# A two-block network on one core: head norms by transposes, retention scores issued a step ahead, three small tiles padded, dense weights split 512 columns at a time

## The chip, the cores and the metric

The kernel runs on one core of a Trainium2 chip. The metric is the device time of one execution, in microseconds (us); the time of a kernel is the median of its runs. TensorE is called PE in the profile, VectorE DVE, ScalarE ACT, GpSimd POOL and SyncE SP.

## The reference, cut to what matters

One sequence of 512 tokens of width 1024 goes through two blocks, all of it in float32. The first block has two layers; each is a mixer and then a feed-forward part, with a layer norm behind each. The mixer projects the tokens and gives each quarter of the width to another recurrence:

```python
p = einsum('btd,dc->btc', h, w_in[l])
pa, pb, pc, pd = _split(p, MIXER_COLS)
ya = _hgrn2_mixer(pa, ...)           # gated linear recurrence, then a norm per head
yb = _gla_mixer(pb, ...)             # the same form, other gates
yc, v_first = _rwkv7_mixer(pc, ...)  # w0 + tanh(w_lr) @ w2, a0 + a_lr @ a2, kk / norm(kk), norm per head
yd = _retnet_mixer(pd, ...)          # (q k^T * decay) v, norm per head
mix = einsum('btc,cd->btd', concatenate([ya, yb, yc, yd]), w_out[l])
h = _layer_norm(DN_ALPHA * h + mix, ...)
f = _swiglu(h, ...) if l == 0 else _moe(h, ...)   # 2816 wide; or 8 experts of 1408, 2 a token
h = _layer_norm(DN_ALPHA * h + f, ...)
```

The norms per head are over 64 values, so a vector of 256 channels has four of them for each token. The second block is a SwiGLU of width 2816, a hybrid mixer (a gated recurrence and a sliding-window attention), and another SwiGLU of width 2816, each with a norm before and behind it.

## The kernel before

**Number format and matmuls.** A float32 product is made of three matmuls of a faster format: every operand is split into a high part and the rest of it (`split`, L350: ScalarE writes `hi` at L352, VectorE `lo` at L353). `mm3` (L381) issues high by high, high weights by low data, low weights by high data (L383 to L385), always with weights of 128x128 and 512 tokens streaming, or 256 where the tokens are taken in halves. `gemm_fm` (L387) sums `nk` such blocks in one PSUM bank; `head_steps` (L433) does the first four outputs of a stage side by side (L443, L444, L446); `gemm_halves` (L404) does the last outputs of a stage with one half of the tokens `lag` blocks behind the other.

**Weights.** A `Stream` (L641) loads raw weights of 128x1024 with SP's queue (L661, a ring of three) and cuts each into pieces of WC=256 columns, each with its own split. Pieces lie in two rings of WB=10 tiles, `whi` and `wlo`, or, for the last units of three stages, in a pool of the stage's own (`wx`). A block of 128 columns is a part of a piece. The experts have a stream of their own (`mhi`, `mlo`, pieces of 1024 columns). Tiles of a pool stand one behind the other in a partition of SBUF, so a small tile's size sets where those behind it begin.

**Stages in time** (us of the profiled execution): mixer of layer 0 to 365, its output projection and layer norm to 415, the first SwiGLU's gate and up projections (operands `xH`, `xL`) to 650 and its down projection (operands `hH`, `hL`) to 765; mixer of layer 1 from 785 to 1140; routing to 1210; eight experts to 1790; second SwiGLU to 2180 (down from 2055 on); hybrid mixer to 2380; third SwiGLU to 2725 (down from 2600 on).

**Order in the mixers of the first block.** `mixer1` (L1489) weaves three chains of generators by costs that their `yield`s state and by weights (`weave`, L782): RWKV (`rwkv_pair` 0 and 1), the projections of all parts, and `hg(0)`, `hg(1)`, `ret`. What is issued on an engine stays in that order. Where all three have work, the projection's large matmuls stand between the small ones of the recurrences.

**What the diff touches there.** `params` (L864) makes small per-channel tiles, `om` the first of them. `head_rstd` (L906) takes squared values `sq` (128 channels, that is two heads, by 512 tokens) and returns in PSUM one factor per head and token, over that head's 64 rows. It is called 10 times in each layer. It sums with four matmuls that use the data as weights (L911), takes Sqrt and reciprocal of 128x8 values (`rstd`, L450: ScalarE L452, VectorE L453; or VectorE's maximum first), and spreads them with eight matmuls by the identity (L922). `self.bones` holds 64x64 blocks of ones on its diagonal; `ident` is the identity. `rwkv_pair` (L1008) makes the decay from one low-rank matmul (`y`, L1021, rows 0 to 63) and, after the decay's chain, the gate from another (L1035, rows 64 to 127). `ret` (L1453) takes pairs of heads j and key tiles jt in turn: scores of two heads on PE, multiplied by a decay matrix `rd` on VectorE (L1471), then two matmuls into `po` (L1474), in the same step.

**The other places.** `tail` is one of the tiles that the router keeps to the end (`Moe.keep`, L1572), and `snk` a small tile of the hybrid mixer in the pool that holds its outputs `yh`, `yl`. The halves of the down projections lie 12 blocks apart (`LAG`, `LAG1`) in the first two SwiGLUs, 18 (`LAG2`) in the third. In `moe_down` the matmul of the rest slots (L2059) has 32 weight columns, in one of four strips of 32 rows in turn.

Of the kernel before, what the change touches and what calls it, by code (L numbers as in the profile page):

```python
# [10 lines left out]
F32R = mybir.dt.float32r  # L11
I32 = mybir.dt.int32
AF = mybir.ActivationFunctionType
OP = mybir.AluOpType
# [4 lines left out]
T = 512  # L19
D = 1024  # L20
P = 128
NT = T // P
# [11 lines left out]
HALF = (slice(0, HT), slice(HT, T))  # L34
WB, WR, WC = 10, 3, 256
HEAD = 4
MR, MW, SHARE = 5, 4, (0, 3, 6)
DECAY_C = math.exp(-0.5)
# [602 lines left out]
class Stream:  # L641
# [22 lines left out]
    def pieces(self, raw):  # L664
        self.units += 1
        return [self.piece(raw[:, c:c + WC]) for c in range(0, 1024, WC)]

    def unit(self):
        return self.ready.pop(0) if self.ready else self.pieces(self.raw())

    def piece(self, raw):
        k = self.K
        if self.pool and self.units > self.own:
            t = self.pool.tile([P, 2, WC], F32R, name="wx", tag="wx", bufs=self.bufs)
            hi, lo = t[:, 0], t[:, 1]
        else:
            hi = k.ws.tile([P, WC], F32R, name="whi", tag="whi", bufs=WB)
            lo = k.ws.tile([P, WC], F32R, name="wlo", tag="wlo", bufs=WB)
        k.split(raw, hi, lo)
        return hi, lo  # L680

    def block(self):
        if self.j == 8:
            self.cur, self.j = self.unit(), 0
        c = self.j * P
        hi, lo = self.cur[c // WC]
        self.j += 1
        return hi[:, c % WC:c % WC + P], lo[:, c % WC:c % WC + P]

# [112 lines left out]
class Mix:  # L802
# [33 lines left out]
    def small(self, n, c):  # L836
        return self.cp.tile([P, c], F32, name=n)
# [26 lines left out]
    def params(self):  # L864
        nc, k, l = self.nc, self.k, self.l
        V = nc.vector
        sm = self.small
        mu = k.par(f"mu{l}")
        self.om = sm("om", 9)
        V.tensor_scalar(self.om, mu, -1.0, 1.0, op0=OP.mult, op1=OP.add)  # L870
# [35 lines left out]
    def head_rstd(self, sq, eps, floor=None):  # L906

        k, nc = self.k, self.nc
        s = k.bankB()
        for i in range(NT):  # L910
            nc.tensor.matmul(s[:, 2 * i:2 * i + 2], sq[:, i * P:(i + 1) * P], k.cA("hsel"), start=True, stop=True)  # L911
        r = k.sm.tile([P, 2 * NT], F32, name="hr")
        if floor is None:
            k.rstd(r, s[:, :2 * NT], eps, 1.0 / 64)
        else:
            nc.vector.tensor_scalar(r, s[:, :2 * NT], floor, None, op0=OP.max)
            nc.scalar.activation(r, r, AF.Sqrt)
            nc.vector.reciprocal(r, r)
        R = k.bankB()
        for i in range(NT):  # L920
            for h in range(2):
                nc.tensor.matmul(R[64 * h:64 * h + 64, i * P:(i + 1) * P],  # L922
                                 r[:, 2 * i + h:2 * i + h + 1].to_broadcast([P, 64]), k.ident, start=True, stop=True)
        return R
# [83 lines left out]
    def rwkv_pair(self, p):  # L1008
# [10 lines left out]
        r, kr = self.x[p], self.x[2 + p]  # L1019
        y = k.bankB()  # L1020
        mm(y, w2[:64, sl], self.x[6][:64], start=True, stop=True)  # L1021
        yield 0.9
        lw = self.a("lw")
        act(lw, y, AF.Tanh, bias=self.hw0[:, p:p + 1], scale=0.5)
# [8 lines left out]
        V.tensor_copy(pe, ch(Pm)[:, :, 63])  # L1033
        y = k.bankB()
        mm(y, w2[64:128, sl], self.x[6][64:128], start=True, stop=True)  # L1035
        yield 0.9
        ta = self.a("ta")
        act(ta, y, AF.Tanh, bias=self.ha0[:, p:p + 1], scale=0.5)
        kt = self.a("kp")
# [413 lines left out]
    def ret(self):  # L1453
# [3 lines left out]
        qk, vt, _ = self.reti  # L1457
        for j in range(2):
            po = k.bankB()
            rd = [self.a("rd") for _ in range(2)]  # L1460
            for h in range(2):
                nc.gpsimd.dma_start(rd[h], k.A["rd"][2 * j + h])
            for jt in range(NT):
                n = T - jt * P
                ss = []
                for h in range(2):
                    rs = slice(64 * h, 64 * h + 64)
                    b = k.bankB()
                    mm(b[:, :n], qk[2 + j][rs, jt * P:(jt + 1) * P], qk[j][rs, jt * P:], start=True, stop=True)
                    s = self.a("Sr")  # L1470
                    V.tensor_tensor(s[:, :n], b[:, :n], rd[h][:, :n], op=OP.mult)  # L1471
                    ss.append(s)
                for h, s in enumerate(ss):
                    mm(po[64 * h:64 * h + 64, jt * P:], vt[:, jt, (2 * j + h) * 64:(2 * j + h + 1) * 64], s[:, :n], start=jt == 0,  # L1474
                       stop=jt == NT - 1, skip_group_check=True)
                yield 1.8
            o, R = self.a("ro"), self.a("rr")
# [87 lines left out]
class Moe:  # L1565
# [37 lines left out]
    def route(self, sT, tot, ap, hot):  # L1603
# [126 lines left out]

        self.tail = self.keep("tail", [P, NT])
        V.tensor_scalar(self.tail, slot[:, :, NE - 1], -float(NS - C), None, op0=OP.add)
# [519 lines left out]
class Hybrid:  # L2252


    def __init__(self, k, s2, big, pool):
# [6 lines left out]
        nc.scalar.dma_start(self.wbd.rearrange("p a b -> p (a b)"), k.A["wbd"])  # L2262
        self.snk = small("snk", 8)
        nc.gpsimd.dma_start(self.snk, k.A["snk"].to_broadcast([P, 8]))
# [269 lines left out]
```

## Time and profile before

| | |
|---|---|
| median of three runs | 2736.74 us (2735.06 to 2743.05) |
| the profiled execution, its own time | 2746.0 us |
| its span, from the first to the last instruction | 2744.2 us |
| its mean granted TensorE clock | 0.982 |
| PE, DVE, ACT, POOL busy | 97%, 61%, 49%, 12% of the span |
| moved by DMA | 333.83 MB, mean 122 GB/s |

The profile is of one execution, a little longer than the median of the three timed ones. Busy time is that in which an engine executes an instruction. Matmuls are pipelined: a record of 0.39 us is followed by the next record some 0.23 us later, so the rate is read from start to start, or by counting records in a window. The name ahead of "MATMUL" is the PSUM tile written, behind the arrow stand the two operands read. A "x4" behind a row of the timeline says that four records in a row were put together. The 40 slices of the page are 68.6 us each.

### The profile page before, as it was taken

To read this page: it belongs to the slowest core of one execution; us is meant where nothing else is said; L and a number is where in the kernel's file an instruction comes from. 1 tells how busy PE (TensorE), PEld (TensorE's weight loads), DVE (VectorE), ACT (ScalarE), POOL (GpSimd) and SP (SyncE) were. 2 spreads that over 40 slices of the span, in tenths; PEclk is the share of its full clock that TensorE was granted. 3 is DMA by queue.
4 is the path that set the end of the run, shared out by engine and by line. 5 is a ranking of instruction groups with operands and counts; after the bars stand their busy time and mean duration, and the time that the engine had idled before them with its cause. 6 is when DMAs were issued, how large, how long until landed. Compare 5 with 4: busy or idle time off the path is not lost. (4 is left out here: it accounts for less than half of the span.)

```text
span 2744.2 us, 48736 instructions
## 1 busy us (share of the span) xinstructions
PE 2661.5 (97%) x18914; PEld 2166.6 (79%) x18914; DVE 1665.4 (61%) x3372; ACT 1335.9 (49%) x2769; POOL 328.1 (12%) x388
## 2 busy tenths in 40 slices
PE   8999999999999999988999999999999999999998
PEld 6777688888877776786888888768888877888887
DVE  7554465443466554456888888965553477755533
ACT  5455335433343553345666777554443367544432
POOL 1000110000030000024333322500000100100000
PEclk9999999999999999989999999989999999999999
DMA  4111413222321112238877777712222212223222
GB/s 165 41 55 48 147 62 101 100 97 95 108 79 41 55 48 70 65 119 272 285 270 271 276 276 274 253 50 100 93 99 93 87 62 65 90 93 100 94 98 70
DMA packets 95788, 333.83 MB, mean 122 GB/s; under 512 B 11825, under 2 KB 15057, under 8 KB 95552
## 3 DMA queue, kind: packets, MB, share of 16 engines
q1 hardware_dynamic: 87424, 306.00, 33.4%
q0 software_dynamic: 7552, 23.96, 2.4%
q8 instruction: 152, 2.49, 0.4%
q10 hardware_dynamic: 576, 0.69, 0.1%
q14 instruction: 84, 0.69, 0.1%
HBM read 313.95 MB, written 17.18 MB: 121 GB/s over the span
## 5 line engine op out<-in xcount | busy, mean ns | idle before, releaser
L352 ACT ACTIVATE whi<-wraw 128x256 fp32r<-128x256 f32 x1164 | 473.5, 415 | 811.8 <-PE bkA L384 751.1
L353 DVE TENSOR_TENSOR wlo<-wraw,whi 128x256 fp32r<-128x256 f32 x1164 | 483.9, 424 | 619.9 <-ACT whi L352 601.5
L383 PE MATMUL bkA<-xH,whi 128*128 128x512 f32 x1352 | 541.4, 400 | 2.6 <-DVE sh L947 2.1
L384 PE MATMUL bkA<-xL,whi 128*128 128x512 f32 x1352 | 533.8, 395 | 0.0
L385 PE MATMUL bkA<-xH,wlo 128*128 128x512 f32 x1352 | 531.9, 393 | 0.0
L1904 PE MATMUL bkA<-xe,mhi 128*128 128x320 f32 x1408 | 365.1, 345 | 3.7 <-ACT mhi L352 2.2
L383 PEld LDWEIGHTS bkA<-xH,whi 128*128 128x128 f32 x1352 | 254.3, 188 | 70.8 <-issue 15.2
L384 PEld LDWEIGHTS bkA<-xL,whi 128*128 128x128 f32 x1352 | 254.7, 188 | 58.2 <-issue 9.6
L385 PEld LDWEIGHTS bkA<-xH,wlo 128*128 128x128 f32 x1352 | 254.5, 188 | 56.3 <-issue 4.2
L1906 PE MATMUL bkA<-xe,mlo 128*128 128x160 f32 x1232 | 292.3, 237 | 3.3 <-DVE mlo L353 3.3
L353 DVE TENSOR_TENSOR mlo<-mraw,mhi 128x1024 fp32r<-128x1024 f32 x165 | 232.9, 1413 | 45.0 <-ACT mhi L352 42.9
L1904 PEld LDWEIGHTS bkA<-xe,mhi 128*128 128x128 f32 x1408 | 254.8, 191 | 5.0 <-ACT mhi L352 2.5
L1906 PEld LDWEIGHTS bkA<-xe,mlo 128*128 128x128 f32 x1232 | 237.5, 193 | 4.7 <-DVE mlo L353 4.5
L383 PE MATMUL bkA<-hH,whi 128*128 128x512 f32 (+1 forms) x548 | 207.0, 378 | 0.0
L384 PE MATMUL bkA<-hL,whi 128*128 128x512 f32 (+1 forms) x548 | 206.7, 377 | 0.0
L385 PE MATMUL bkA<-hH,wlo 128*128 128x512 f32 (+1 forms) x548 | 206.5, 377 | 0.0
L352 ACT ACTIVATE mhi<-mraw 128x1024 fp32r<-128x1024 f32 x165 | 173.2, 1052 | 18.5 <-PE bkA L2066 14.6
L353 DVE TENSOR_TENSOR mlo<-wraw,mhi 128x1024 fp32r<-128x1024 f32 x99 | 131.4, 1327 | 33.8 <-ACT mhi L352 31.3
L384 PEld LDWEIGHTS bkA<-hL,whi 128*128 128x128 f32 x548 | 103.0, 188 | 21.0
L383 PEld LDWEIGHTS bkA<-hH,whi 128*128 128x128 f32 x548 | 103.0, 188 | 21.0
L385 PEld LDWEIGHTS bkA<-hH,wlo 128*128 128x128 f32 x548 | 102.9, 188 | 20.9
L352 ACT ACTIVATE mhi<-wraw 128x1024 fp32r<-128x1024 f32 x99 | 104.5, 1056 | 13.0 <-PE bkA L2066 7.7
(717 smaller groups left out, 4414.3 us busy)
## 6 DMA issues: line engine op xcount, KB each, us to landing
mraw<-moew SPq DMA_DIRECT2D x165, 512.0 KB, 5.3
wraw<-moew SPq DMA_DIRECT2D x99, 512.0 KB, 4.5
wraw<-win SPq DMA_DIRECT2D x76, 512.0 KB, 3.7
wraw<-f0gu SPq DMA_DIRECT2D x44, 512.0 KB, 3.2
wraw<-f1gu SPq DMA_DIRECT2D x44, 512.0 KB, 3.3
wraw<-f2gu SPq DMA_DIRECT2D x44, 512.0 KB, 3.3
wraw<-f0d SPq DMA_DIRECT2D x22, 512.0 KB, 3.7
wraw<-f1d SPq DMA_DIRECT2D x22, 512.0 KB, 3.3
```

The source lines that it names most:

```text
L352: nc.scalar.activation(hi, x, AF.Copy)
L353: nc.vector.tensor_tensor(lo, x, hi.bitcast(F32), op=OP.subtract)
L383: mm(ps, wH, xH, start=first, stop=False)
L384: mm(ps, wH, xL, start=False, stop=False)
L385: mm(ps, wL, xH, start=False, stop=last)
L1904: mm(ps, wH, xf[:, q], start=q == 0, stop=last, skip_group_check=True)
L1906: mm(ps[:, :C], wL, xe[:, q, 0], start=False, stop=False, skip_group_check=True)
```

## The change

Three constants change: pieces of dense weights have 512 columns (`WC`) in rings of five (`WB`), so that a ring holds the same bytes; pieces in a stage's own pool keep 256 (`XC`). Three small tiles are made 8 floats longer (`GRAIN`), of which only the part that was there is used: `om` in layer 0, `tail`, `snk`. `head_rstd` sums with the ones as weights and the data streaming, each 128 tokens into its own 32 rows of one bank; ScalarE copies the 128x128 sums, PE transposes them, VectorE scales (or takes the maximum) and inverts 128x8 values, ScalarE takes the Sqrt and writes each value 64 times, and four PE transposes bring that to channels by tokens. `rwkv_pair` issues both low-rank matmuls together, into two banks, and the gate's Tanh ahead of the decay's. `ret` issues the scores of a step and VectorE's product before the `po` matmuls of the step ahead of it; the loads of the next pair's `rd` go out with the first scores of that pair.

```diff
@@ -32,8 +32,9 @@
 LIM = CAP
 HT = T // 2
 HALF = (slice(0, HT), slice(HT, T))
-WB, WR, WC = 10, 3, 256
+WB, WR, WC, XC = 5, 3, 512, 256
 HEAD = 4
+GRAIN = 8
 MR, MW, SHARE = 5, 4, (0, 3, 6)
 DECAY_C = math.exp(-0.5)
 
@@ -663,15 +664,17 @@
 
     def pieces(self, raw):
         self.units += 1
-        return [self.piece(raw[:, c:c + WC]) for c in range(0, 1024, WC)]
+        own = self.pool and self.units > self.own
+        n = XC if own else WC
+        return [self.piece(raw[:, c:c + n], own) for c in range(0, 1024, n)]
 
     def unit(self):
         return self.ready.pop(0) if self.ready else self.pieces(self.raw())
 
-    def piece(self, raw):
+    def piece(self, raw, own):
         k = self.K
-        if self.pool and self.units > self.own:
-            t = self.pool.tile([P, 2, WC], F32R, name="wx", tag="wx", bufs=self.bufs)
+        if own:
+            t = self.pool.tile([P, 2, XC], F32R, name="wx", tag="wx", bufs=self.bufs)
             hi, lo = t[:, 0], t[:, 1]
         else:
             hi = k.ws.tile([P, WC], F32R, name="whi", tag="whi", bufs=WB)
@@ -682,10 +685,10 @@
     def block(self):
         if self.j == 8:
             self.cur, self.j = self.unit(), 0
-        c = self.j * P
-        hi, lo = self.cur[c // WC]
+        c, n = self.j * P, 1024 // len(self.cur)
+        hi, lo = self.cur[c // n]
         self.j += 1
-        return hi[:, c % WC:c % WC + P], lo[:, c % WC:c % WC + P]
+        return hi[:, c % n:c % n + P], lo[:, c % n:c % n + P]
 
 
 class MoeStream(Stream):
@@ -866,7 +869,7 @@
         V = nc.vector
         sm = self.small
         mu = k.par(f"mu{l}")
-        self.om = sm("om", 9)
+        self.om = sm("om", 9 + (0 if l else GRAIN))[:, :9]
         V.tensor_scalar(self.om, mu, -1.0, 1.0, op0=OP.mult, op1=OP.add)
         self.hw0, self.ha0, self.hka, self.oka = sm("hw0", 2), sm("ha0", 2), sm("hka", 2), sm("oka", 2)
         V.tensor_scalar(self.hw0, k.par(f"w0{l}"), 0.5, None, op0=OP.mult)
@@ -906,21 +909,25 @@
     def head_rstd(self, sq, eps, floor=None):
 
         k, nc = self.k, self.nc
-        s = k.bankB()
+
+        s = k.bankB()[:, :P]
         for i in range(NT):
-            nc.tensor.matmul(s[:, 2 * i:2 * i + 2], sq[:, i * P:(i + 1) * P], k.cA("hsel"), start=True, stop=True)
+            nc.tensor.matmul(s[32 * i:32 * i + 32], self.bones[:, 48:80], sq[:, i * P:(i + 1) * P], start=True, stop=True)
+        rows, rb = sq[:, :P], sq
+        nc.scalar.activation(rows, s, AF.Copy)
+        st = k.bankB()[:, :P]
+        nc.tensor.transpose(st, rows, k.ident)
+        st = st.rearrange("p (n c) -> p n c", c=16)[:, :, 0]
         r = k.sm.tile([P, 2 * NT], F32, name="hr")
         if floor is None:
-            k.rstd(r, s[:, :2 * NT], eps, 1.0 / 64)
+            nc.vector.tensor_scalar(r, st, 1.0 / 64, eps, op0=OP.mult, op1=OP.add)
         else:
-            nc.vector.tensor_scalar(r, s[:, :2 * NT], floor, None, op0=OP.max)
-            nc.scalar.activation(r, r, AF.Sqrt)
-            nc.vector.reciprocal(r, r)
+            nc.vector.tensor_scalar(r, st, floor, None, op0=OP.max)
+        nc.vector.reciprocal(r, r)
+        nc.scalar.activation(rb.rearrange("p (n c) -> p n c", c=64), r[:, :, None].to_broadcast([P, 2 * NT, 64]), AF.Sqrt)
         R = k.bankB()
         for i in range(NT):
-            for h in range(2):
-                nc.tensor.matmul(R[64 * h:64 * h + 64, i * P:(i + 1) * P],
-                                 r[:, 2 * i + h:2 * i + h + 1].to_broadcast([P, 64]), k.ident, start=True, stop=True)
+            nc.tensor.transpose(R[:, i * P:(i + 1) * P], rb[:, i * P:(i + 1) * P], k.ident)
         return R
 
     def head_center(self, o):
@@ -1017,9 +1024,12 @@
         b8 = lambda a: a.rearrange("p (c f) -> p c f", f=64)
         yield from self.wait(lambda: all(j in self.x for j in (p, 2 + p, 6)))
         r, kr = self.x[p], self.x[2 + p]
-        y = k.bankB()
+        y, ya = k.bankB(), k.bankB()
         mm(y, w2[:64, sl], self.x[6][:64], start=True, stop=True)
+        mm(ya, w2[64:128, sl], self.x[6][64:128], start=True, stop=True)
         yield 0.9
+        ta = self.a("ta")
+        act(ta, ya, AF.Tanh, bias=self.ha0[:, p:p + 1], scale=0.5)
         lw = self.a("lw")
         act(lw, y, AF.Tanh, bias=self.hw0[:, p:p + 1], scale=0.5)
         V.tensor_scalar(lw, lw, -0.5 * DECAY_C, -0.5 * DECAY_C, op0=OP.mult, op1=OP.add)
@@ -1031,11 +1041,6 @@
         act(Pm, cum, AF.Exp)
         pe = self.cp.tile([P, 8], F32, name=f"pe{p}")
         V.tensor_copy(pe, ch(Pm)[:, :, 63])
-        y = k.bankB()
-        mm(y, w2[64:128, sl], self.x[6][64:128], start=True, stop=True)
-        yield 0.9
-        ta = self.a("ta")
-        act(ta, y, AF.Tanh, bias=self.ha0[:, p:p + 1], scale=0.5)
         kt = self.a("kp")
         V.tensor_scalar(kt, ta, self.hka[:, p:p + 1], self.oka[:, p:p + 1], op0=OP.mult, op1=OP.add)
         V.tensor_tensor(kt, kt, kr, op=OP.mult)
@@ -1455,25 +1460,39 @@
         V, mm, act = nc.vector, nc.tensor.matmul, nc.scalar.activation
         yield from self.wait(lambda: self.reti)
         qk, vt, _ = self.reti
-        for j in range(2):
-            po = k.bankB()
-            rd = [self.a("rd") for _ in range(2)]
-            for h in range(2):
-                nc.gpsimd.dma_start(rd[h], k.A["rd"][2 * j + h])
-            for jt in range(NT):
-                n = T - jt * P
-                ss = []
+        steps = [(j, jt) for j in range(2) for jt in range(NT)]
+        rd = {}
+
+        def scores(j, jt):
+
+            if jt == 0:
+                rd[j] = [self.a("rd") for _ in range(2)]
                 for h in range(2):
-                    rs = slice(64 * h, 64 * h + 64)
-                    b = k.bankB()
-                    mm(b[:, :n], qk[2 + j][rs, jt * P:(jt + 1) * P], qk[j][rs, jt * P:], start=True, stop=True)
-                    s = self.a("Sr")
-                    V.tensor_tensor(s[:, :n], b[:, :n], rd[h][:, :n], op=OP.mult)
-                    ss.append(s)
-                for h, s in enumerate(ss):
-                    mm(po[64 * h:64 * h + 64, jt * P:], vt[:, jt, (2 * j + h) * 64:(2 * j + h + 1) * 64], s[:, :n], start=jt == 0,
-                       stop=jt == NT - 1, skip_group_check=True)
-                yield 1.8
+                    nc.gpsimd.dma_start(rd[j][h], k.A["rd"][2 * j + h])
+            n = T - jt * P
+            bs, ss = [k.bankB()[:, :n] for _ in range(2)], []
+            for h, b in enumerate(bs):
+                rs = slice(64 * h, 64 * h + 64)
+                mm(b, qk[2 + j][rs, jt * P:(jt + 1) * P], qk[j][rs, jt * P:], start=True, stop=True)
+            for h, b in enumerate(bs):
+                s = self.a("Sr")[:, :n]
+                V.tensor_tensor(s, b, rd[j][h][:, :n], op=OP.mult)
+                ss.append(s)
+            return ss
+
+        nxt = scores(*steps[0])
+        yield 0.9
+        for c, (j, jt) in enumerate(steps):
+            ss, nxt = nxt, scores(*steps[c + 1]) if c + 1 < len(steps) else None
+            yield 0.7
+            if jt == 0:
+                po = k.bankB()
+            for h, s in enumerate(ss):
+                mm(po[64 * h:64 * h + 64, jt * P:], vt[:, jt, (2 * j + h) * 64:(2 * j + h + 1) * 64], s, start=jt == 0,
+                   stop=jt == NT - 1, skip_group_check=True)
+            yield 0.9
+            if jt < NT - 1:
+                continue
             o, R = self.a("ro"), self.a("rr")
             act(o, po, AF.Copy)
             self.head_center(o)
@@ -1728,7 +1747,7 @@
             V.tensor_reduce(gg, tmp, axis=AX.X, op=OP.add)
             self.gts.append(gg)
 
-        self.tail = self.keep("tail", [P, NT])
+        self.tail = self.keep("tail", [P, NT + GRAIN])[:, :NT]
         V.tensor_scalar(self.tail, slot[:, :, NE - 1], -float(NS - C), None, op0=OP.add)
         self.govf = self.keep("govf", sh)
         V.tensor_tensor(self.govf, gate, ok, op=OP.mult)
@@ -2260,7 +2279,7 @@
         nc.scalar.dma_start(self.cc, k.A["cc"])
         self.wbd = big.tile([P, 8, P], F32, name="wbd")
         nc.scalar.dma_start(self.wbd.rearrange("p a b -> p (a b)"), k.A["wbd"])
-        self.snk = small("snk", 8)
+        self.snk = small("snk", 8 + GRAIN)[:, :8]
         nc.gpsimd.dma_start(self.snk, k.A["snk"].to_broadcast([P, 8]))
         self.hb, self.c4 = k.hb, k.c4
         self.Rs = s2.scale_rows(big)
```

## Rows read from the trace of the kernel before

**Rows 1.** The page: busy time by engine, and PE's row of the 40 slices.

```profile
PE 2661.5 (97%) x18914; PEld 2166.6 (79%) x18914; DVE 1665.4 (61%) x3372; ACT 1335.9 (49%) x2769; POOL 328.1 (12%) x388
...
PE   8999999999999999988999999999999999999998
```

**Rows 2.** Waits: line, awaited, us in total, times, longest (PE's; then all).

```profile
PE bkA L443 <- ACT whi L352: 7.5, 2, 6.5
...
PE bkB L1474 <- DVE Sr L1471: 2.9, 8, 0.9
...
ACT whi L352 <- PE bkA L384: 751.1, 782, 7.0
```

**Rows 3.** Windows of PE, first gate/up and down: length, busy (matmuls), clock, DMA.

```profile
450.00:640.00 190.00, 190.00 (x840) 1.00 0.30 97
655.00:745.00 90.00, 90.00 (x388) 1.00 0.32 108
```

**Rows 4.** Timeline of PE: output projections, first and last of 19 and 9.

```profile
365.68 0.39 PE L383 MATMUL bkA<-yH,whi 128*128 128x512 f32 x1
...
369.80 0.39 PE L383 MATMUL bkA<-yH,whi 128*128 128x512 f32 x1
...
1131.87 0.40 PE L385 MATMUL bkA<-yH,wlo 128*128 128x512 f32 x1
...
1133.73 0.40 PE L384 MATMUL bkA<-yL,whi 128*128 128x512 f32 x1
```

**Rows 5.** Timeline of PE: experts' down matmuls, first and last of nine.

```profile
1346.46 0.39 PE L2065 MATMUL bkA<-mhi,hid 128*128 128x512 f32 x1
...
1348.29 0.40 PE L2067 MATMUL bkA<-mlo,hid 128*128 128x512 f32 x1
```

**Rows 6.** Groups of PE by line and form (one of three alike).

```profile
L383 PE MATMUL bkA<-hH,whi 128*128 128x512 f32 x460 | 181.9, 396 | 0.0
```

**Rows 7.** Timeline of one head norm: PE's, ScalarE's and VectorE's instructions of it.

```profile
152.02 1.05 PE L911 MATMUL bkB<-ca,gn 128*128 128x2 f32 x8
152.94 0.48 PE L384 MATMUL bkA<-xL,whi 128*128 128x512 f32 x1
153.26 0.39 PE L385 MATMUL bkA<-xH,wlo 128*128 128x512 f32 x1
...
155.19 1.09 PE L922 MATMUL bkB<-ca,hr 128*64 128x128 f32 x16
156.22 0.70 PE L1241 MATMUL bkB<-sh,pm 128*128 128x512 f32 x1
...
151.99 1.28 ACT L452 ACT_TABLE_LOAD   x1
153.28 0.27 ACT L452 ACTIVATE hr<-bkB,eps 128x8 f32<-128x8 f32 x1
...
153.58 0.20 DVE L453 RECIPROCAL hr<-hr 128x8 f32<-128x8 f32 x1 [1.68 <-ACT hr L452]
```

**Rows 8.** Timeline of PE: sixteen L2059 records to L2065; four transposes to L858.

```profile
1343.80 0.62 PE L2059 MATMUL bkB<-mraw,rest 128*32 128x512 f32 x2
...
1345.65 0.50 PE L2065 MATMUL bkA<-mhi,hid 128*128 128x512 f32 x1
...
80.14 0.60 PE L1001 MATMUL bkB<-ca,kk 128*128 128x128 f32 x4
80.49 0.36 PE L858 MATMUL bkA<-whi,xH 128*128 128x256 f32 x1
```

**Rows 9.** Timeline of PE: low-rank matmul, second pair of layer 0.

```profile
161.04 1.12 PE L1021 MATMUL bkB<-sh,pm 64*128 64x512 f32 x2
```

**Rows 10.** Groups of the page and by form: splits of 256 and 512 columns.

```profile
L352 ACT ACTIVATE whi<-wraw 128x256 fp32r<-128x256 f32 x1164 | 473.5, 415 | 811.8 <-PE bkA L384 751.1
...
L352 ACT ACTIVATE hH<-su 128x512 fp32r<-128x512 f32 x44 | 27.8, 631 | 2.0
```

**Rows 11.** Window of PE in layer 0's mixer: at a low clock.

```profile
58.00:66.00 8.00, 7.08 (x114) 0.57 0.07 28
```

## The prediction, made before the change was run

> **What bounds the kernel now.** First the page's totals and slices: TensorE (PE) is busy 97% of the 2744.2 us, VectorE 61%, ScalarE 49%, and PE's row shows 8 or 9 in each of the 40 slices [rows 1]. Then the waits of PE, longest first: the first is 7.5 us, in two pieces, and none of the others is longer [rows 2]. So time comes off this kernel only where PE's own instructions take less, or where one of those waits goes. The counts of matmuls in steady stretches say what one 512-column matmul costs: 190 us hold 840 of them in the first gate/up stage, 90 us hold 388 in the first down stage [rows 3]. A record lasts 0.39 us [rows 4], so some 1.7 of those counted stand across the edges of a window: 190 / 838.3 is 226.7 ns from start to start, 90 / 386.3 is 233.0. The two later pairs of stages agree to within one matmul. Both at a granted clock of 1.00, the 2.4 GHz level. In the slices of the mixers (to 350 us, and 785 to 1140) PE shows 9 as well, so a matmul saved there is time saved too.
>
> **Padding.** The pads add 8 floats, 32 bytes of a partition, to three small tiles; what matters is where later tiles then start. In the program compiled from the kernel before, xH, whi and wlo start at multiples of 64 bytes, yh, yl and layer 0's yH, yL too; hH, hL, layer 1's yH, yL and all of the experts' tiles start 32 bytes past one. `tail` moves everything behind it by 32 bytes, `om` (layer 0 only) and `snk` put layer 0's y and the second block's yh back where they were. After it both operands of every large matmul start on 64. Rows that show what that is worth: moving operand and weights both on 64, 226.7 ns; the moving one 32 off, 233.0 [rows 3]. Layer 0's output projection (both on 64) takes 4.12 us for 18 starts, 228.9 ns; layer 1's (32 off) 1.86 us for eight, 232.5 [rows 4]. With both operands 32 off the experts' down matmuls take 1.83 us for eight, 228.8 ns [rows 5], so it is unlike starts that cost. Counts: 460 hH matmuls in each of three lines [rows 6], 1380 x 6.3 ns = -8.7 us, nothing else bounding those stretches. Layer 1's projection: 192 x 3.6 = -0.7. The 264 halves of 256 columns in the last two FFNs change the other way about: by the same 3.6 ns and half the length some 0.5 us, of either sign; 0 taken. The 528 experts' matmuls: between 0 and -1.1 (228.8 to 226.7); 0 taken. Sum **-9.5**; bounds -11 and 0.
>
> The 233.0 ns row is against a rule of the Trainium skill, page "SBUF — State Buffer", section "Specifications (TRN2)": it gives lines of 16 bytes, and either start is a whole number of them; "TensorE: Matmul & The Clock Gate", section "Back-to-back issue gap", gives the gap by the number of columns alone. By these two the padding is worth 0, which is the second rival below; the trace differs, 233.0 against 226.7 ns at 512 columns.
>
> **Head norms.** `head_rstd` runs 20 times, 10 in each layer. One call now: eight L911 records from 152.02 to 152.94, 0.92 us, then sixteen L922 records from 155.19 to 156.22, 1.03 us [rows 7]; 1.95 us of PE. (There are four and eight matmuls in the code: each leaves two records.) L911 loads 128 data columns as weights to stream 2. The change loads 32 columns of ones and streams 128, into four different 32-row strips. No row shows just this; the nearest is the experts' L2059, also 32 weight columns in four strips, at 512 columns: sixteen records in 1.85 us [rows 8], so eight at 128 columns are 0.23 us if length scales; the other bound is today's 0.92. I take 0.35, near the first, since the shape is that of L2059, plus its edges. The new transpose of the row sums and the four at the end: four L1001 transposes take 0.35 us [rows 8], 0.09 each; the first is a visit of PE by itself, and entering and leaving a small group costs some 0.1 us each (152.94 to 153.26 is 0.32 against 0.23 [rows 7]): 0.3 and 0.45. New sum 1.1, saved 0.85, less 0.1 for a new hop that comes late: 0.75 x 20 = **-15**. Bounds: 0.23 + 0.09 + 0.35 = 0.67, so -26; and 0, if waits eat it.
>
> What the hop adds: a ScalarE copy of 128x128 behind the matmuls (0.3 us, between 0.27 for 8 columns [rows 7] and 0.415 for 256 [rows 10]), then PE's transpose, two VectorE instructions of 0.2 us, a Sqrt that writes 512 columns instead of 8 (0.63 for 0.27 us, as the 512-column split [rows 7, 10]). The Sqrt still brings one table load of 1.28 us [rows 7], and the transpose and the VectorE work fall beside it. Behind the copy on ScalarE stand weight splits; behind PE's transpose stand the projection's matmuls, in order. Those splits are early (below), so a late copy delays PE only by its own lateness. The consumer (VectorE's multiply) gets R some 0.5 us later per call; the two other interleaved chains cover it.
>
> **Retention.** Now PE waits for VectorE's score product: 2.9 us in eight waits [rows 2]. The scores of the next step issued ahead take them away; the two POOL-queue loads of `rd` for the second pair go out earlier, and two more score banks and four more tiles are live at the end, when the RWKV chain no longer needs them. **-3**; bounds -5 and +1. What is late next is the step's own matmul, already in order.
>
> **RWKV.** The `ya` matmul moves beside `y`. In layer 0's second pair the first stands alone, 1.12 us of PE in two records [rows 9], and so does the second; `w2`'s upper and lower halves are rows 64 to 127 and 0 to 63 of PE, so side by side both take about the time of one. In the three other pairs they already come together. So **-1**, once; bounds -2 and +1 (one more bank held). The Tanh of `ta` moves ahead of that of `lw` on ScalarE: 0.6 us later for the decay, hidden by the projections' matmuls.
>
> **Pieces of 512.** 582 splits instead of 1164. ScalarE: 2 x 415 becomes 631 ns (the 512-column split of hH) [rows 10], 116 us less work; VectorE likewise. It is worth **0**: ScalarE's splits wait 751 us for PE to give a slot back [rows 2], so weights are ready long before use, and the ring holds 20 blocks as before. Without that cover each stage start would wait 0.2 us more for hi and as much again for lo. At the end of the last FFN, whose halves lie 18 blocks apart, the last piece of four gets its slot only when two blocks of the second half are done; PE has those and later ones to do, 0 to +1. Bounds -2 and +3.
>
> **Sum:** -9.5 - 15 - 3 - 1 = -28.5 us. The profiled execution took 2746.0 (2744.2 of span and 1.8 around it), 9.3 above the median of 2736.74; so 2717.5 for a run like it, and **2708** against the median. All lower bounds at once (-11 - 26 - 5 - 2 - 2) give 2691, all upper ones (+5) 2742; between 2691 and 2722 I hold the forecast itself for met.
>
> **Rivals.** (1) The norms and the mixers give nothing back: PE's saved time turns into short waits on the longer chain. For it: the mixers' PE sits in order, and ScalarE and VectorE are half busy there. Against it: today's waits there are small [rows 2]. Then only the padding counts: 2727. Chance 0.20. (2) The start of the tile is not what makes 233.0, or is undone elsewhere: only the mixers count, 2736.7 - 19 = 2718. It is what the two pages of the Trainium skill named above would make of the padding. Against it: the rows of four stages sort by their starts [rows 3 to 5]. Chance 0.09. (3) Slower: PE's transposes are put straight behind their inputs, and PE stands through copy, table load, long Sqrt and VectorE: 0.3 + 1.28 + 0.6 + 0.4 = 2.6 us in each of 20 calls, +52 - 28.5, so 2760. It decides from 1.4 us a call on (28.5/20). Against it: today other matmuls lie between the two groups for 2.2 us [rows 7]. Chance 0.12, a quarter of it near no change. More than my bounds: 0.04. The forecast itself: 0.55.
>
> **Numbers.** 0.3% is 8.2 us, about what a measurement of this kernel can tell from no change: faster ends at 2728.5. Faster: 0.55 + 0.04 + 0.09 + half of rival 1 = 0.78; same: the other half and a quarter of rival 3 = 0.13; slower 0.09. Range 2691 to 2734: it takes in rivals 1 and 2 and leaves out rival 3 and the 0.04.
>
> **Clock.** A stretch of 8 us in layer 0's mixer has a mean granted clock of 0.57, so some 6.9 us at the 1.2 GHz level, among PE's smallest matmuls [rows 11]; there is a second like it at 96 us. One more or less is half of that, 3.4 us, of either sign; that is within the bounds.
>
> **What would show it.** Right: 397 matmuls in 90 us of each down stage instead of 388; L911's place taken by short groups of under 0.4 us; PE's wait for Sr gone; ScalarE busy some 100 us less, with no change of PE in gate/up. Wrong: down stages still at 233; new waits of PE for ScalarE's copy or Sqrt above 0.3 us a call; both mixers together not 10 us shorter.

## The result, and the profile after

The changed kernel takes 2701.82 us (median of four runs, 2698.7 to 2708.82) against 2736.15 us before (four runs, 2735.06 to 2743.05): the ratio is 0.9873, its 95% interval 0.9846 to 0.9899, so 34 us less. The forecast was 2708. The profiled execution took 2699.64 us, with a span of 2697.9. The page's busy times and PE's row, which answer to [rows 1]:

```profile
PE 2617.8 (97%) x18694; PEld 2142.6 (79%) x18694; DVE 1585.4 (59%) x2806; ACT 1252.3 (46%) x2207; POOL 331.2 (12%) x388
...
PE   8999999999999999988999999899999999999998
```

PE is still at 97%: of the 46.3 us between the two spans 43.7 are PE's busy time, so hardly any of it came from waits. Not all of the 43.7 is less work: some 9 us are a higher granted clock in the experts' combine (32.51 us of PE before, 23.92 after for the same matmuls, experiments 11 and 12). Where the rest went is read stage by stage. The windows of the first gate/up stage and of the three down stages (length, PE busy and count, clock, DMA), to be held against [rows 3]:

```profile
440.00:620.00 180.00, 180.00 (x796) 1.00 0.30 97
640.00:730.00 90.00, 90.00 (x399) 1.00 0.33 110
2020.00:2110.00 90.00, 90.00 (x399) 1.00 0.30 100
2575.00:2665.00 90.00, 90.00 (x398) 1.00 0.28 91
```

This gate/up stage is unchanged (180 / 794.3 is 226.6 ns); the down stages hold 399 matmuls in 90 us where there were 388, again 226.5 ns after taking 1.7 off the count as before. One head norm, of the call that answers to [rows 7] (PE's and ScalarE's timelines; start, duration, line):

```profile
146.34 0.43 PE L915 MATMUL bkB<-gn,ca 128*32 128x128 f32 x8
146.70 0.50 PE L385 MATMUL bkA<-xL,whi 128*128 128x512 f32 x1
147.03 0.39 PE L386 MATMUL bkA<-xH,wlo 128*128 128x512 f32 x1
...
147.73 0.30 PE L919 MATMUL bkB<-ca,gn 128*128 128x128 f32 x1
147.78 0.47 PE L386 MATMUL bkA<-xH,wlo 128*128 128x512 f32 x1
148.10 0.39 PE L384 MATMUL bkA<-xH,whi 128*128 128x512 f32 x1
...
150.85 0.60 PE L930 MATMUL bkB<-ca,gn 128*128 128x128 f32 x4
151.28 1.02 PE L1246 MATMUL bkB<-sh,pm 128*128 128x512 f32 x2
...
147.38 0.27 ACT L917 ACTIVATE gn<-bkB 128x128 f32<-128x128 f32 x1
148.66 1.28 ACT L927 ACT_TABLE_LOAD   x1 [1.01 <-DVE hr L926]
149.95 0.63 ACT L927 ACTIVATE gn<-hr 128x512 f32<-128x512 f32 x1
```

PE gives this call 0.36 us for the sums, 0.05 for the lone transpose (and 0.09 more for the matmul behind it, 0.32 where 0.23 is usual), and 0.43 for the last transposes: 0.93 where it was 1.95. From ScalarE's copy to the end of the Sqrt 3.2 us pass, and PE fills them with the projection's matmuls.

Of PE's waits the first one was 7.5 us in [rows 2] (that wait, now at L444, is 8.2); the waits for `Sr` are gone from the list:

```profile
PE bkB L1144 <- issue: 8.2, 7, 2.4
PE bkA L444 <- ACT whi L353: 8.2, 2, 6.9
PE bkB L1818 <- DMA gslot<-gg: 5.9, 1, 5.9
PE bkA L2086 <- DVE mlo L354: 4.3, 3, 2.0
```

The splits in groups, against [rows 10]:

```profile
L353 ACT ACTIVATE whi<-wraw 128x512 fp32r<-128x512 f32 x582 | 365.2, 630 | 752.0 <-PE bkA L385 695.8
L354 DVE TENSOR_TENSOR wlo<-wraw,whi 128x512 fp32r<-128x512 f32 x582 | 399.9, 690 | 499.0 <-ACT whi L353 488.9
```

ScalarE's splits take 108 us less and still wait 696 us for PE. The stages, from one stage's first matmul to the next one's, in us (two executions of each kernel; the second ones are experiments 11 and 12):

| stage | before | before, again | after | after, again |
|---|---|---|---|---|
| mixer 0, to its output projection | 333.6 | 327.8 | 320.7 | 321.0 |
| output projection 0 and the mixer's rest | 61.1 | 61.1 | 58.0 | 58.0 |
| FFN 0 gate/up, down | 243.0, 127.9 | 243.1, 127.9 | 243.2, 124.8 | 243.1, 124.8 |
| mixer 1 | 337.8 | 337.0 | 332.1 | 330.4 |
| output projection 1, routing | 101.8 | 98.6 | 92.2 | 91.9 |
| experts and their combine | 602.3 | 602.3 | 591.7 | 594.5 |
| FFN 1 gate/up, down | 241.4, 126.3 | 241.4, 126.3 | 241.4, 124.7 | 241.4, 124.7 |
| hybrid mixer, its output projection | 130.5, 49.5 | 130.5, 49.5 | 127.5, 53.4 | 127.4, 53.3 |
| FFN 2 gate/up, down | 245.5, 126.8 | 245.5, 126.8 | 247.2, 123.9 | 247.2, 123.9 |

Two executions of one kernel differ by up to 6 us in mixer 0 and 3 in the routing, and by nothing in the dense stages. The two mixers together take 652.8 and 651.4 us where they took 671.4 and 664.8, so 12 to 20 us less.

The granted clock moves these lengths both ways. Before, 17.1 and 6.8 us of the two mixers and 45.1 and 45.0 us of the experts were at the lower level, 1.2 GHz; after, 30.7 and 37.5 us of the mixers and 23.4 and 26.0 of the experts. Counted at half for time at the lower level, an estimate of the length at 2.4 GHz throughout, the mixers fall from 662.9 and 661.4 us to 637.5 and 632.6, and the experts do not fall (579.7 twice before, 580.0 and 581.5 after). So the change took some 24 to 30 us of work from the mixers and lost a part of it to the clock there, and what the experts gained is clock alone (experiments 11 and 12).

### The profile page after: what moved, and what is told of

The parts are those of the page before. It is cut to its first block, busy times and chain, and to the rows that moved or that the text cites. A ratio compares the mean times of both kernels' runs of the same rounds, so it can differ in the third digit from the quotient of the medians.

```text
span 2697.9 us, 46430 instructions
## 1 busy us (share of the span) xinstructions
PE 2617.8 (97%) x18694; PEld 2142.6 (79%) x18694; DVE 1585.4 (59%) x2806; ACT 1252.3 (46%) x2207; POOL 331.2 (12%) x388
## 5 line engine op out<-in xcount | busy, mean ns | idle before, releaser
L353 ACT ACTIVATE whi<-wraw 128x512 fp32r<-128x512 f32 x582 | 365.2, 630 | 752.0 <-PE bkA L385 695.8
L354 DVE TENSOR_TENSOR wlo<-wraw,whi 128x512 fp32r<-128x512 f32 x582 | 399.9, 690 | 499.0 <-ACT whi L353 488.9
L354 DVE TENSOR_TENSOR mlo<-mraw,mhi 128x1024 fp32r<-128x1024 f32 x165 | 232.9, 1414 | 45.1 <-ACT mhi L353 43.8
```

Of the source, the lines that this page charges most:

```text
L353: nc.scalar.activation(hi, x, AF.Copy)
L354: nc.vector.tensor_tensor(lo, x, hi.bitcast(F32), op=OP.subtract)
```

## The experiments

**1 to 4: one part of the change alone.** Each is the kernel before with one group of the diff's hunks: the three pads; `head_rstd`; `Stream` with `WB`, `WC`, `XC`; `ret` and `rwkv_pair`.

> The kernel before with the three pads alone. Theory (unlike starts cost): the three down stages fall from 233 to 226.7 ns a matmul, each shorter by 2.5 to 3 us, layer 1's output projection by 0.7 us; together -9 us, so about 0.9965 of the time before, and nothing else moves. Rival 2 (starts are not what makes 233): ratio 1.000, down stages still at 233 ns. A third case: the change's surplus of 6 us over my sum comes from the padding, through the experts or the combine behind them; then -15 us, 0.9945.

> The kernel before with the new head_rstd alone. Theory: PE's part of a call falls from 1.95 us to some 0.95 (groups of 0.36, 0.14 and 0.43 us in the changed kernel's trace), so -0.75 to -1.0 us a call, -15 to -20 us in all: ratio 0.9927 to 0.9945. Rival 1 (given back as short waits): ratio 0.998 to 1.000. Rival 3 (PE stands through the new hop): above 1.000.

> The kernel before with pieces of 512 columns in rings of five alone. Theory (weights are ready long before use): 1.000, within 0.1%, with ScalarE some 108 us less busy and VectorE some 84. Rival: the shorter queues of ScalarE and VectorE let the mixers' small operations start earlier, -3 to -6 us (0.998), seen in the mixers and not in the dense stages. Other rival: coarser slots delay the stage starts, +3 us (1.001), seen at the first matmul of each stage and at the end of the last down stage.

> The kernel before with the retention's scores a step ahead and the two low-rank matmuls side by side, the rest unchanged. Theory: PE's wait for the score product (2.9 us) is gone and one low-rank matmul of 1 us shares PE: -4 us, ratio 0.9985. Rival: another wait takes its place (the next in the order), 1.000. Other rival: the added banks delay the chains beside it, above 1.000.

| part | ratio to before | 95% interval | in us of 2736 | predicted | span x clock, us |
|---|---|---|---|---|---|
| pads | 0.9967 | 0.9951 to 0.9983 | -9.0 | -9.5 | -9.1 |
| head norms | 0.9928 | 0.9902 to 0.9955 | -19.7 | -15 | -22.2 |
| pieces of 512 | 0.9993 | 0.9981 to 1.0005 | -1.9 | 0 | +0.7 |
| retention, RWKV | 0.9985 | 0.9969 to 1.0002 | -4.1 | -4 | -11.7 |

The last column is the difference to before of the mean product of each run's span and mean granted clock (2691.4 us over 30 runs of before), an estimate of what is left when the clock is taken out; for the whole change it is -39.0 (2652.4). Within one kernel this product varies less than the time.

The product of the four ratios is 0.9873, the ratio of the whole change. The parts' intervals together leave some 10 us either way, so the agreement to the last digit is luck; it shows that the parts roughly add up, and the last column (-42.3 against -39.0) says the same. With the pads alone the down stages fall from 127.9 to 124.8, from 126.3 to 123.4 and from 126.8 to 123.9 us, so rival 2 is out. Rival 1 is out as well: the norms' interval stays clear of no gain, and in their profile the two mixers take 644.8 us against 671.4 and 664.8.

**5 and 6: which starts cost.** That the pads act on the down stages doesn't show that the rule of 64 bytes was right, and the output projections speak against it. Layer 0's has both operands on 64 before and after; by the rule of 64 alone it ought to have stayed at 229 ns [rows 4] or come to 226.7. It got slower, 29 starts in 6.74 us, 232.4 ns (timeline of PE after, first and last of 30):

```profile
351.18 0.39 PE L384 MATMUL bkA<-yH,whi 128*128 128x512 f32 x1
...
357.92 0.40 PE L386 MATMUL bkA<-yH,wlo 128*128 128x512 f32 x1
```

In the compiled programs its `yH` starts 64 bytes past a multiple of 256 before and 128 past one after; xH starts on 256 always, hH 224 past before and on 256 after. Experiment 5 moves hH and hL of the changed kernel by 64, 128 and 32 bytes in the three FFNs (`off` is 32 and 8 floats in the second and third; the line of the first, not shown, has 16 in its place), experiment 6 spreads the weights' slots.

```diff
-            hH = p.tile([P, NH, T], F32R, name="hH")
+            off = 32 if n == 1 else 8
+            hH = p.tile([P, NH * T + off], F32R, name="hH")[:, off:].rearrange("p (b t) -> p b t", t=T)
```

> The changed kernel with hH and hL moved by 64 bytes in the first FFN, 128 in the second, 32 in the third (xH, whi, wlo stay). My prediction's rule (unlike starts modulo 64 cost): down stages at 226.7, 226.7 and 233 ns a matmul. Rival rule, read off the output projections after the change (moving operand 128 past a multiple of 256 bytes: 232; 64 past: 229; 32 past: 229 to 230; on it: 226.7): 229 to 230, 232 and 229 to 230. Third: no rule of starts, 226.7 in all three.

```profile
635.00:725.00 90.00, 90.00 (x395) 1.00 0.31 105
2025.00:2115.00 90.00, 90.00 (x387) 1.00 0.29 94
2585.00:2675.00 90.00, 90.00 (x387) 1.00 0.26 85
```

These windows of its three down stages give 228.8, 233.6 and 233.6 ns, after the same 1.7. So 64 past a multiple of 256 costs 2 ns, 128 past costs 7 although it is a multiple of 64: the prediction's rule falls. 32 past costs 7 as well, not the 2 to 3 that I had read off the experts, whose weights stood elsewhere too.

Experiment 6 (cut: a second hunk makes the small tile `invf` 192 bytes longer, which keeps the moving operands where they were):

```diff
-            hi = k.ws.tile([P, WC], F32R, name="whi", tag="whi", bufs=WB)
-            lo = k.ws.tile([P, WC], F32R, name="wlo", tag="wlo", bufs=WB)
+            hi = k.ws.tile([P, WC + 8], F32R, name="whi", tag="whi", bufs=WB)[:, :WC]
+            lo = k.ws.tile([P, WC + 8], F32R, name="wlo", tag="wlo", bufs=WB)[:, :WC]
```

> The changed kernel with the ten slots of whi and wlo 32 bytes further apart, so that the weights' starts go through 0, 32, ... 224 past multiples of 256 while every moving operand stays where it was. My prediction's rule (unlike starts): gate/up matmuls with weights 32 or 96 past cost 233 instead of 226.7, so the gate/up stages get 3 to 7 us longer each. Rival rule (only the moving operand's start counts): 226.7 for all of them, stages as before to 0.3 us.

```profile
440.00:620.00 180.00, 180.00 (x777) 1.00 0.29 96
```

777 matmuls where the changed kernel has 796 in the same window: 232.2 ns on the mean, and the gate/up stages are 248.3, 246.9 and 251.0 us long, 4 to 6 more. So the weights' start counts too, and the rival rule as I had put it (the moving operand alone) falls as well. What both runs bear out for the dense stages: 226.7 ns when both operands start on a multiple of 256 bytes, and 229 to 236 in the mixtures tried otherwise (experiment 6 by means of four starts on one weight tile). A formula for the mixtures I don't have.

**7: everything on 256.** The changed kernel with more padding (`om` by 128 bytes in both layers, `snk` by 192, two tiles of the experts by 128 and 64), so that the operands of all large matmuls start on 256.

```diff
-        self.om = sm("om", 9 + (0 if l else GRAIN))[:, :9]
+        self.om = sm("om", 9 + 4 * GRAIN + (0 if l else GRAIN))[:, :9]
...
-        self.snk = small("snk", 8 + GRAIN)[:, :8]
+        self.snk = small("snk", 8 + 7 * GRAIN)[:, :8]
...
```

> The changed kernel with more padding, so that the moving operands of the three output projections and of the experts also start at multiples of 256 bytes. Rule of 256: output projections of both layers from 232 to 227 ns a matmul (192 each: -1 us each), the hybrid's from 229 to 227 (-0.5), the experts' 528 down matmuls from 229.7 to 227 (-1.6); 4 us less than the changed kernel, ratio to the kernel before 0.9858 if that one is at 0.9873. Rule of 64 (all these start on 64 already): no change, 0.9873.

2700.21 us (2697.2 to 2703.07), ratio 0.9863 (0.9825 to 0.9901). Layer 0's projection, the same 29 starts as above, takes 6.57 us, 226.6 ns:

```profile
351.31 0.39 PE L386 MATMUL bkA<-yH,wlo 128*128 128x512 f32 x1
...
357.88 0.39 PE L385 MATMUL bkA<-yL,whi 128*128 128x512 f32 x1
```

There the rate is as the rule of 256 has it. The experts' down matmuls, on 256 in this run too, did not follow: 230.0 ns on the mean of their starts where the change has 229.7, with ten starts at 226 ns and nine at 232 in one stage:

```profile
1320.18 0.39 PE L2085 MATMUL bkA<-mhi,hid 128*128 128x512 f32 x1
...
1322.44 0.39 PE L2086 MATMUL bkA<-mlo,hid 128*128 128x512 f32 x1
...
1325.11 0.40 PE L2085 MATMUL bkA<-mhi,hid 128*128 128x512 f32 x1
...
1327.20 0.39 PE L2085 MATMUL bkA<-mhi,hid 128*128 128x512 f32 x1
```

So starts are not all that sets the rate there; what else does was not found. The gain of 1.6 us in the medians (4 expected) is less than the runs can tell, so this version isn't shown to be faster than the change.

**8 and 10: what a us of PE in a head norm is worth.** The changed kernel with the four sum matmuls issued twice, and six times.

```diff
-        for i in range(NT):
+        for i in [i for _ in range(6) for i in range(NT)]:
             nc.tensor.matmul(s[32 * i:32 * i + 32], self.bones[:, 48:80], sq[:, i * P:(i + 1) * P], start=True, stop=True)
```

> The changed kernel with the four sum matmuls of every head norm issued twice (the second time into the same place with the same values). Theory (PE's instructions in the mixers are the bound): 0.36 us x 20 = 7 us longer than the changed kernel, ratio to the kernel before 0.990. Rival (PE has slack there and the chain through ScalarE and VectorE is the bound): within 2 us of the changed kernel, 0.9873 to 0.988.

> The changed kernel with the four sum matmuls of every head norm issued six times. Five extra groups of 0.22 us (what a second one measured) are 1.1 us of PE a call, 22 us in all. Theory (PE's instructions bound the mixers): 18 to 24 us longer than the changed kernel, ratio to the kernel before 0.994 to 0.996. Rival (the chains through ScalarE and VectorE bound the mixers, PE has slack): under 8 us longer, below 0.990.

Twice: 2703.7 us, ratio 0.9867 (0.9827 to 0.9906). A second group costs PE 0.22 us, not 0.36 (the 0.36 holds the edges of the group), 4.4 us in all: 2 us more than the changed kernel in the medians, inconclusive. Six times: 2719.17 us (2704.84 to 2722.86), ratio 0.9923 (0.9894 to 0.9952). The group then lasts from 144.66 to 146.10 in this call, 1.45 us; the row below is a window of the experts' combine in the same run:

```profile
144.66 1.52 PE L915 MATMUL bkB<-gn,ca 128*32 128x128 f32 x48
146.10 0.50 PE L385 MATMUL bkA<-xL,whi 128*128 128x512 f32 x1
```

```profile
1753.00:1790.00 37.00, 35.41 (x121) 0.72 0.19 58
```

All 20 groups together hold PE for 28.9 us (start of a group to start of what follows) where the change has 7.1: 21.8 us more PE gave 17.4 us more time by the medians, 14 by the ratios. The stages of its profile don't put these us into the mixers alone. The mixers are only 8 to 9.5 us longer than after the change (660.9), with 17.1 us at the lower clock where the change has 30.7 and 37.5; the experts are 9.5 to 12 us longer (604.0), by the clock of the window above. Span times clock, which takes that out, gives 17.4 us more (2669.8 against 2652.4) here, and 1 us less in experiment 8 (2651.4). So PE has no slack for 22 us of work: some 0.8 of a us of PE is a us of work by experiment 10, as an estimate. What is left of it in the time depends on the clock, and for a few us it isn't shown.

**9: a late hop.** ScalarE's copy made eight times in every norm.

```diff
-        nc.scalar.activation(rows, s, AF.Copy)
+        for _ in range(8):
+            nc.scalar.activation(rows, s, AF.Copy)
```

> The changed kernel with ScalarE's copy of the sums made eight times in every head norm (the same values into the same place), so that the new hop comes some 1.9 us later (7 x 0.27). Theory (other chains' matmuls stand behind the sums on PE and cover the hop): 0 to 8 us longer than the changed kernel, ratio to the kernel before 0.987 to 0.990. Rival 3's mechanism (PE stands in order through the hop): 20 x 1.9 = 38 us longer, ratio above 1.000.

2699.13 us, ratio 0.986 (0.9834 to 0.9886): no longer than the change. In one call the copies take from 140.37 to 143.19, and PE's transpose comes right behind them; until 142.77 other matmuls start:

```profile
140.37 2.13 ACT L918 ACTIVATE gn<-bkB 128x128 f32<-128x128 f32 x7
142.92 0.27 ACT L918 ACTIVATE gn<-bkB 128x128 f32<-128x128 f32 x1
...
142.77 0.39 PE L386 MATMUL bkA<-xH,wlo 128*128 128x512 f32 x1
143.24 0.33 PE L920 MATMUL bkB<-ca,gn 128*128 128x128 f32 x1
```

The hop has more than 2 us of cover in a call; rival 3's mechanism isn't there.

**11 and 12: the clock in the experts' combine.** The experts' stage is 8 to 11 us shorter after the change, where the prediction had no gain at all. The kernel before and the changed one, unaltered, were profiled again.

> The kernel before, profiled once more. If the stretch at half the clock in the experts' combine (20 us long in the trace of before, gone in the trace after) belongs to the kernel, it is there again; if it comes and goes from run to run, it is gone or shorter here, and the 9 us between the two traces there are no effect of the change.

> The changed kernel, profiled once more. If the half-clock stretch in the experts' combine comes and goes from run to run, it may be there now (this execution then some 9 us longer than 2699, near 2709); if it belongs to the kernel, it is absent again and the time is near 2700. The down stages, the head norms' groups and the hybrid's wait for yh (2.1 us) should be as in the first profile, to 0.1 us, either way.

Windows of the last expert's end and the combine, of before, before again, after, after again:

```profile
1778.00:1814.00 36.00, 32.51 (x110) 0.72 0.14 46
```

```profile
1768.00:1804.00 36.00, 33.20 (x113) 0.72 0.15 46
```

```profile
1743.00:1769.00 26.00, 23.92 (x110) 1.00 0.17 54
```

```profile
1745.00:1771.00 26.00, 23.41 (x109) 1.00 0.15 45
```

The same 110 matmuls (a few records are missing in each) take 36 us at a mean clock of 0.72 in both profiles of before, and 26 us at 1.00, the 2.4 GHz level, in both of after. It isn't the change as such, though: the stretch is there with the pads alone, and in experiments 9 and 10, which contain the whole change; it isn't there in experiments 2 to 8. What decides it was not found. Some 10 us of an execution hang on it. Both profiles of before have the stretch and neither of the changed kernel has it, so of the 34 us between the medians up to 10 can be this and not less work; the experiments' medians contain it to an unknown part.

**What the pieces do in the hybrid mixer.** In the changed kernel, and with the pieces alone, the hybrid mixer is 3 us shorter and its output projection 4 us longer. The timeline of PE after shows why the first is given back:

```profile
2278.66 1.20 PE L384 MATMUL bkA<-yh,whi 128*128 128x512 f32 x4 [2.14 <-ACT yh L353]
2279.91 0.80 PE L385 MATMUL bkA<-yl,whi 128*128 128x512 f32 x1
2280.51 0.63 PE L386 MATMUL bkA<-yh,wlo 128*128 128x512 f32 x1
2280.93 0.63 PE L384 MATMUL bkA<-yh,whi 128*128 128x512 f32 x1
2281.36 0.63 PE L385 MATMUL bkA<-yl,whi 128*128 128x512 f32 x1
```

The projection begins earlier and comes to the last yh, which the recurrence has not yet made; PE stands 2.1 us, and the matmuls that follow come 0.43 us apart instead of 0.23: the clock is at its lower level, 1.2 GHz, until 2283. Before, the projection waited there for a weight split 1.1 us, and the clock stayed at 1.00. A second stretch of 3.4 us at the lower level follows at 2341, in the third SwiGLU's gate/up stage, and makes it 1.7 us longer (247.2 for 245.5), after the change as with the pieces alone. In both, too, the first matmul of the hybrid mixer comes 1.3 us later than with 256 columns, which the table books to the second down stage: that is why it fell by 1.6 us and not by the 2.9 of the pads.

## Why the prediction was right, and where its steps were not

**What bounds the kernel, and the sum.** Right in the main: PE's own work bounds the kernel, and the parts roughly add up. Not right is that time comes off "only where PE's own instructions take less, or where one of those waits goes": the experts got 8 to 11 us shorter by the granted clock alone, and in the mixers the clock took some of the gain back. The prediction's term for the clock, 3.4 us of either sign, was too small: the experts' stretch of 20.5 us at the lower level is worth 10 us, and the mixers have 14 to 31 us more at it than before, 7 to 15 us. The time is 6 us below the forecast. By span times clock the work fell by 39 us for the 28.5 forecast, with the norms at 22 for 15 and retention and RWKV at 12 for 4; that the time came out so near is partly luck, since the clock took back a part of this surplus.

**Padding.** The size was right (-9.0 for -9.5), the rule was not. The step that failed is "it is unlike starts that cost", with its multiples of 64: the three rows that I had sorted by it (0 and 0, 0 and 32, 32 and 32) sort as well by 256, and the fourth, layer 0's projection at 228.9 with both on 64, already fitted badly. hH happened to come to a multiple of 256, so the down stages' term held by luck. Layer 0's projection, for which I took no change, lost some 3 ns a matmul, and layer 1's, for which I took 3.6 ns, gained 1 (from 233.5 to 232.3 on the mean of its matmuls' starts); both are worth under 1 us. Why the experts' matmuls stay near 230 with everything on 256 is open. What the prediction said of the two pages of the Trainium skill holds: neither lines of 16 bytes ("SBUF — State Buffer", "Specifications (TRN2)") nor a gap by columns alone ("TensorE: Matmul & The Clock Gate", "Back-to-back issue gap") gives 226.7 and 233 ns for the same 512 columns, and here the measurement decides.

**Head norms.** Right in mechanism and sign; the term was too small. I had 1.1 us for the new PE work and took 0.1 off for a late hop. Measured are 0.88 us for the three groups on the mean of 20 calls (0.36, 0.04, 0.48) and 0.09 for the edge of the lone transpose, which I had priced at 0.3 in all; before it was 1.91. The late hop costs nothing (experiment 9). 0.94 x 20 is 19 us, and experiment 2 has 19.7 in time and 22 by span times clock. The row that the sums were priced by was the right one: a second group costs 0.22, and 0.23 stood in the prediction as the length scaled from [rows 8].

**Retention and RWKV.** -4.1 for -4 in time, with an interval that reaches to 0; the wait for `Sr` is gone and none stands in its place. That the number was met is luck: by span times clock this part took off 12 us, and its runs lost 47.5 us to the clock (span less that product) where before lost 40.2. Where the 8 us beyond the forecast's 4 came from was not found. The two parts were not tried one by one.

**Pieces.** 0 within the interval, as predicted, with ScalarE's splits 108 us shorter for 116. ScalarE as a whole is only 84 us less busy, since copies and wide Sqrts of the norms came in. The place where I looked for a cost, the last piece behind the 18 blocks' lag, shows none (the last stage's length is that of the pads alone, 123.9). The cost is in the hybrid's output projection and, by the clock, in the stage behind it, which I had covered by "weights are ready long before use": true of weights, but the projection's data were not ready.

**What would show it.** 397 in 90 us was given, 399, 399 and 398 came; the figure left out the 1.7 at the edges. The sums are under 0.4 us a call, ScalarE is 84 us less busy for "some 100", and gate/up is unchanged but for the 1.7 us of the third. Of the signs of being wrong none came: the two mixers are 12 to 20 us shorter, where under 10 would have been one.

## What to carry to other kernels

Where one kind of matmul runs at two rates in two stages, compare the start addresses of its operands: a pad of 32 bytes in a small tile ahead of them moved 1380 matmuls from 233 to 226.7 ns. Ask for a rule with several starts in one run before trusting it, since three rows fitted two rules here. Hold the granted clock of each stage, or span times clock of each run, beside the times: a part that took 12 us of work off showed as 4 in time here. In a stage that PE fills in order, price a change of a helper by PE's start-to-start time of its groups with their edges, and let other chains cover the rest. Where a stage ends in a chain of its own, as the hybrid mixer does, a gain ahead of it can come back: here 3 us did, as 2.1 us of waiting and a lower clock.

## What the hardware showed that I had not expected

A matmul of 512 columns took 226.7 ns with both operands' starts on multiples of 256 bytes in the dense stages and up to 236 otherwise, and the weights' start counted as much as the moving operand's: 232.2 on the mean with weights spread over multiples of 32. The experts' matmuls stayed at 230 with both on 256. A lone 128-column transpose put between large matmuls took 0.05 us of PE and 0.09 at its edge. And the same combine code ran in 26 or in 36 us by the granted clock alone, in kernels that differ only elsewhere.
